# Side products grouped into runs, cheaper norms of k, and refitted plan costs in a float32 DeltaNet/HGRN2 trunk

## Chip, cores and metric

The kernel runs on one core of one Trainium2 chip. The metric is the device time of one launch in microseconds (us). Three runs of the kernel before took 2888.34 to 2891.47 us, median 2890.0.

## What is computed

Two decoder layers over 256 tokens of width 2048, all in float32. Layer 0 mixes tokens with a gated DeltaNet (GDN), layer 1 with HGRN2; a SwiGLU follows each, and an RMSNorm ends the trunk. Cut to what matters here:

```python
def gdn_mixer(h, w_in, ...):                 # 16 key heads, 32 value heads of 128
    proj = h @ w_in                          # k, q, v, z and two gates
    qkv = silu(causal_depthwise_conv(proj[..., :8192], conv_w))
    q, k = l2norm(q) * 128 ** -0.5, l2norm(k)   # x * rsqrt(sum(x * x) + 1e-6)
    A = where(strict, (k b) @ k.T * decay, 0)   # per chunk of 64 tokens
    T = triangular_solve(eye + A, eye)          # its inverse
    ...                                         # o from T, v, decayed q k.T
    return (rmsnorm(o, head_norm) * silu(z)) @ w_out

def swiglu(h, w_gate, w_up, w_down):
    return (silu(h @ w_gate) * (h @ w_up)) @ w_down
```

HGRN2 forms its scores from products of q and k whose decay differs per channel; the kernel builds them in levels (spans of 64, 32, 16, ... tokens).

## The kernel before

**Main stream.** Every weight matrix is read once, in 946 pieces of 512 KB. SyncE issues the reads; ScalarE rounds a piece to fp32r (`wh`), VectorE takes the rest (`wl = raw - wh`). Each float32 product is then three fp32r products of TensorE (high by high, high by low, low by high). Products of weights with the activations go into tiles called `main` (two of them in PSUM), in the fixed order of the groups: for GDN `GDN_ORDER`, where k3, v3 and z3 are the projections of head group 3 (2 key heads, 4 value heads) and o0 to o3 the output projection, each over two head groups; then the FFN, HGRN2, the second FFN. One piece is 12 products of 512 columns or 24 of 256.

**Side products.** All else on TensorE goes into tiles called `aux` (four in PSUM): transposes (`head` holds the identity), scores of k and q (`kqv`), sums of squares (`ones,sq`), the block inverse (`inv`, `u`, `nmat`), outputs (`r`, `w`, `v`, `sc`), HGRN2 scores (`qp`, `kp`, `q_last`).

**Inverse of a head group.** `gdn_qk` multiplies the scores with the decay into `nmat`. `gdn_inverse` (L931) writes its 32x32 diagonal blocks to DRAM (`n_dram`), reads them back spread over the partitions (`wide`, 512 KB), inverts them by 31 pairs of VectorE instructions (the recurrence, `utmp` and `u`), writes the result to DRAM (`u_dram`), reads it into `u`, transposes blocks into `inv` on VectorE, and finishes with 32x32 and 64x64 products on TensorE. The four kinds of transfer stand in one queue, that of POOL, in program order, as do the reads and writes of the residual `x`.

**What sets the order.** All calls are first recorded (`Recorder`), then `plan` (L274) simulates five engines with the costs of `COST`, `LANDING` and `MARGIN` and writes each engine's program in the order that comes out. On TensorE a side product is put ahead of the next main product once its inputs are planned to be ready, plus `HOP` and `PE_SLACK` (1.5 us). The engines then run these lists in order, and wait on semaphores where an input is late. All instructions are issued from one line, L439, so rows are told apart by the names of their tiles.

Of the kernel before, what the change touches and what calls it, by code (L numbers as in the profile page):

```python
# [11 lines left out]
AF = mybir.ActivationFunctionType  # L12
ALU = mybir.AluOpType
PSUM = bass.MemoryType.PSUM
# [3 lines left out]
P = 128  # L18
T = 256
D = 2048  # L20
EPS = 1e-6
CH = 64
# [10 lines left out]
GDN_ORDER = (  # L33
    "k0 k1 v0 z0 v1 k2 z1 k3 v2 z2 v3 k4 o0 z3 k5 v4 k6 o1 v5 k7 z4 z5 v6 z6 v7 z7 o2 o3"
)
# [5 lines left out]
HOP = 0.2  # L41
PE_SLACK = 1.5
FP32_PRODUCT = 0.224
COST = {
    ("vector", "tensor_tensor"): (0.14, 1.08e-3),
    ("vector", "scalar_tensor_tensor"): (0.20, 1.08e-3),
    ("vector", "tensor_scalar"): (0.16, 0.7e-3),
# [6 lines left out]
    ("vector", "reciprocal"): (0.20, 1.0e-3),  # L54
    ("scalar", "activation"): (0.22, 0.83e-3),
# [3 lines left out]
    ("gpsimd", "affine_select"): (0.5, 1.1e-3),  # L59
}  # L60
MARGIN = 1.06
POW = 1.75
LANDING_OF = {"wide": 15.0}
TABLE = {AF.Exp: "exp", AF.Silu: "silu", AF.Sigmoid: "sigmoid", AF.Ln: "ln", AF.Tanh: "exp silu sigmoid"}
# [72 lines left out]
class Recorder:  # L137
# [134 lines left out]


    def plan(self):  # L274
        ops = self.ops
        for op in ops:
            for p in op.pred:
                p.succ.append(op)
# [17 lines left out]
        order = []  # L296
        table = None
        starved = {}
# [45 lines left out]
        while len(order) < len(ops):  # L344
# [15 lines left out]
            if e == "scalar" and op.method == "activation":  # L360
                need = TABLE.get(op.args[2])
                if need and table not in need.split():
                    table = need.split()[0]
                    op.cost += TABLE_LOAD
            self.at[op.n] = at
            order.append(op)
# [84 lines left out]
class Trunk:  # L451
# [162 lines left out]
    def make_xt(self, cg, norm):  # L614
        nc = self.nc
        for pair in range(2):
            ps = self.aux()
            for k in range(2):
                for tt in range(2):
                    nc.tensor.transpose(  # L620
                        ps[:, k * T + tt * P : k * T + (tt + 1) * P],
                        self.x[cg][:, tt, (2 * pair + k) * P : (2 * pair + k + 1) * P],
                        self.ident,
                    )
            for k in range(2):
# [220 lines left out]
    def gdn_qk(self, hg, pre, st):  # L846
# [33 lines left out]
        for kh in range(2):  # L880
# [22 lines left out]
            nc.vector.tensor_scalar(  # L903
                out=ss[:, kh, :], in0=ps1[:, T : T + 4], scalar1=1e-6, scalar2=None, op0=ALU.add
            )
# [95 lines left out]
    def gdn_v(self, hg, pre, st):  # L1001
        nc = self.nc
        v = self.tile(self.pool, [P, 4, T], "kqv")
        self.conv_silu(pre, [32 + 4 * hg + h for h in range(4)], v)
        r = self.tile(self.pool, [P, 2, 4, P], "r")
        for tt in range(2):
            tr = self.aux()
            for h in range(4):
                nc.tensor.transpose(
                    tr[:, h * P : (h + 1) * P], v[:, h, tt * P : (tt + 1) * P], self.ident  # L1010
                )
            for kh in range(2):
# [18 lines left out]
    def head_out(self, o, zs, scale, norm):  # L1031
# [40 lines left out]
        oh, ol = (t([P, 4, T], f"ot_{x}", dt=F32R, bufs=3) for x in "hl")  # L1072
        for b in range(2):
            tr = self.aux()
            for h in range(2):
                for tt in range(2):
                    nc.tensor.transpose(
                        tr[:, h * T + tt * P : h * T + (tt + 1) * P],
                        og[:, tt, (2 * b + h) * P : (2 * b + h + 1) * P], self.ident,
                    )  # L1080
            s = slice(2 * b, 2 * b + 2)
# [189 lines left out]
    def hgrn_scores(self, g, q, st):  # L1271
# [34 lines left out]
        nc.gpsimd.memset(sc, 0.0)  # L1306
        for n, s in enumerate(LEVELS[:-1]):
            e, qp = t([P, 4, T], "e", bufs=2, ordered=True), t([P, 4, P], "qp", bufs=2, ordered=True)
# [16 lines left out]
            tt(qp.rearrange("p h (n s) -> p (h n) s", s=s), qv[:, :, 1, :], ev[:, :, 1, :], ALU.mult)  # L1325
            ps = self.aux()
            for h in range(4):
                for tok in range(2):
# [4 lines left out]
                        qp[:, h, tok * CH : (tok + 1) * CH], start=True, stop=True,  # L1333
                    )
            pv = ps.rearrange("p (a n s) -> p a n s", a=8, s=s)
            if whole:
                for i in range(CH // s):
# [4 lines left out]
            else:  # L1342
# [5 lines left out]
                )  # L1348


        e, qp = t([P, 4, T], "e", bufs=2, ordered=True), t([P, 8, CH + P], "q_last")
# [5 lines left out]
        tt(qp[:, :, 0:CH], qv[:, :, :, 1], ev[:, :, :, 1], ALU.mult)  # L1357
        mask = lambda m: m.unsqueeze(1).broadcast_to([P, 2, m.shape[1]])
        for h in range(4):
            ps = self.aux()  # L1360
            pv = ps[:, 0 : 2 * (CH + P)].rearrange("p (a i) -> p a i", a=2)
            for tok in range(2):
                nc.tensor.matmul(
                    pv[:, tok, :], k[:, h, tok * P : (tok + 1) * P], qp[:, 2 * h + tok, :],
                    start=True, stop=True,
                )
            out = sc[:, 2 * h : 2 * h + 2, :]
            nc.vector.copy_predicated(
                out.rearrange("p a (n t) -> p a n t", t=2)[:, :, :, 1],
                mask(self.masks[:, len(MASKED) - 1, :]), pv[:, :, 0:CH],  # L1370
            )
            nc.vector.copy_predicated(out, mask(self.same), pv[:, :, CH:])
        st["sc"] = sc
# [188 lines left out]
```

## Time and profile before

| | |
|---|---|
| median of three runs | 2890.0 us |
| profiled execution | 2890.57 us |
| its span | 2888.8 us |
| PE / DVE / ACT / POOL busy | 2851.6 / 1717.8 / 1430.9 / 197.3 us |
| mean granted TensorE clock | 0.995 |
| main products | 9024 of 512 columns, 4656 of 256 |
| runs of side products between main products | 350 |

Matmuls overlap, and the end of one is modelled, so durations on PE are not to be added up. The distance from one start to the next is what a product takes in the stream. A product of two float32 operands stands as two records (x8 is four products); a transpose and an fp32r product stand as one.

### The profile page before, as it was taken

The numbers are of one execution on the slowest core, as the hardware profiler recorded it, in microseconds if no ns is written. First come the engines' busy times: TensorE is split into PE (matmuls) and PEld (weight loads), VectorE is DVE, ScalarE is ACT, GpSimd is POOL, SyncE is SP. The second block draws the span as 40 slices with busy tenths as digits, with TensorE's granted clock in tenths as the row PEclk, the third lists the DMA queues.
The fourth block names the chain that finished last, engine by engine and source line by source line (L and its number), as shares of the span: only waits on it lengthen the run. The fifth ranks groups of instructions, "written<-read, shape, count | busy, mean of one in ns | idle before, by whom it ended". The sixth has DMA issues, their size and how long they took to land.

```text
span 2888.8 us, 41300 instructions
## 1 busy us (share of the span) xinstructions
PE 2851.6 (99%) x16074; PEld 2461.4 (85%) x16074; DVE 1717.8 (59%) x2477; ACT 1430.9 (50%) x1998; POOL 197.3 (7%) x286
## 2 busy tenths in 40 slices
PE   8999999999999999999999999999999999999998
PEld 8999979798888888888888989989888888888886
DVE  6777766677755554444445577677665545444454
ACT  6646556456555444434444555556454444344443
POOL 1101111221010000000000100000010000000000
PEclk9999999999999999999999999999999999999999
DMA  7565565755567555666556645445585556665554
GB/s 240 187 190 162 178 193 164 218 169 162 168 224 235 190 189 189 204 229 199 190 189 216 216 148 176 151 148 176 188 283 190 189 188 201 226 205 190 190 199 150
DMA packets 158004, 555.96 MB, mean 192 GB/s; under 512 B 21216, under 2 KB 21360, under 8 KB 157680
## 3 DMA queue, kind: packets, MB, share of 16 engines
q1 hardware_dynamic: 137456, 498.23, 52.7%
q0 software_dynamic: 19264, 53.00, 5.9%
q8 instruction: 126, 2.06, 0.3%
q10 hardware_dynamic: 1088, 2.10, 0.2%
q14 instruction: 70, 0.57, 0.1%
HBM read 530.14 MB, written 23.10 MB: 192 GB/s over the span
## 4 chain that ended last, share of the span: by engine, by line
PE 96%; DMA 2%; issue 1%; DVE 0%; ACT 0%; POOL 0%; ACTq 0%; POOLq 0%; DVEq 0%
PE main L439 88%; PE aux L439 8%; DMA u<-u_dram 1%; DMA u_dram<-u 1%; DMA x<-in_x 0%; ACT wh L439 0%; DVE wl L439 0%; DVE y L439 0%; ACT junk L439 0%; POOL x L439 0%; DVE inv L439 0%; DVE x L439 0%; ACT xt_h L439 0%; ACT kqv L439 0%; DVE xt_l L439 0%
## 5 line engine op out<-in xcount | busy, mean ns | idle before, releaser
L439 DVE TENSOR_TENSOR wl<-raw,wh 128x1024 fp32r<-128x1024 f32 x946 | 1159.3, 1226 | 1045.9 <-ACT wh L439 1045.0
L439 ACT ACTIVATE wh<-raw 128x1024 fp32r<-128x1024 f32 x946 | 1002.7, 1060 | 1294.5 <-PE main L439 1214.1
L439 PE MATMUL main<-wl,xt_h 128*128 128x512 f32 x1920 | 754.7, 393 | 0.0
L439 PE MATMUL main<-wh,xt_l 128*128 128x512 f32 x1920 | 754.7, 393 | 0.0
L439 PE MATMUL main<-wh,xt_h 128*128 128x512 f32 x1920 | 752.4, 392 | 0.0
L439 PE MATMUL main<-xt_h,wh 128*128 128x256 f32 x1552 | 445.4, 287 | 0.0
L439 PE MATMUL main<-xt_l,wh 128*128 128x256 f32 x1552 | 444.2, 286 | 0.0
L439 PE MATMUL main<-xt_h,wl 128*128 128x256 f32 x1552 | 442.8, 285 | 0.2 <-DVE wl L439 0.2
L439 PEld LDWEIGHTS main<-wh,xt_l 128*128 128x128 f32 x1920 | 360.9, 188 | 75.4 <-issue 0.2
L439 PEld LDWEIGHTS main<-wh,xt_h 128*128 128x128 f32 x1920 | 360.7, 188 | 73.7 <-issue 0.7
L439 PEld LDWEIGHTS main<-wl,xt_h 128*128 128x128 f32 x1920 | 360.6, 188 | 73.1 <-issue 0.7
L439 PEld LDWEIGHTS main<-xt_l,wh 128*128 128x128 f32 x1552 | 298.5, 192 | 2.8 <-issue 1.9
L439 PEld LDWEIGHTS main<-xt_h,wh 128*128 128x128 f32 x1552 | 298.5, 192 | 2.0 <-issue 1.2
L439 PEld LDWEIGHTS main<-xt_h,wl 128*128 128x128 f32 x1552 | 298.3, 192 | 1.7 <-issue 0.7
L439 PE MATMUL main<-wl,hth 128*128 128x512 f32 x704 | 274.3, 390 | 0.0
L439 PE MATMUL main<-wh,htl 128*128 128x512 f32 x704 | 274.2, 390 | 0.0
L439 PE MATMUL main<-wh,hth 128*128 128x512 f32 x704 | 274.2, 389 | 0.0
L439 PEld LDWEIGHTS main<-wh,htl 128*128 128x128 f32 x704 | 132.2, 188 | 27.6
L439 PEld LDWEIGHTS main<-wh,hth 128*128 128x128 f32 x704 | 132.2, 188 | 27.4
L439 PEld LDWEIGHTS main<-wl,hth 128*128 128x128 f32 x704 | 132.2, 188 | 27.1
L439 PE MATMUL main<-wh,ot_h 128*128 128x512 f32 x384 | 153.0, 399 | 0.0
L439 PE MATMUL main<-wh,ot_l 128*128 128x512 f32 x384 | 152.4, 397 | 0.0
(181 smaller groups left out, 2196.7 us busy)
## 6 DMA issues: line engine op xcount, KB each, us to landing
raw<-in_ffn_gu SPq DMA_DIRECT2D x352, 512.0 KB, 3.6
raw<-in_ffn_d SPq DMA_DIRECT2D x176, 512.0 KB, 4.2
raw<-in_hgrn_in SPq DMA_DIRECT2D x128, 512.0 KB, 3.6
raw<-in_gdn_kq SPq DMA_DIRECT2D x64, 512.0 KB, 3.8
raw<-in_gdn_v SPq DMA_DIRECT2D x64, 512.0 KB, 4.4
raw<-in_gdn_z SPq DMA_DIRECT2D x64, 512.0 KB, 3.6
raw<-in_gdn_out SPq DMA_DIRECT2D x64, 512.0 KB, 3.9
x_home<-x POOLq DMA_DIRECT2D x36, 512.0 KB, 4.7
```

Of the source, the lines that this page charges most:

```text
L439: getattr(getattr(tc.nc, op.eng), op.method)(*args, **kw)
```

## The change

1. `batches()` runs before the plan: the products into one `aux` tile, or into two tiles that were allocated `together`, are tied so that all become ready for the plan at once, when the last input of any is. Transposes, HGRN2 levels and last-level products are rewritten into such pairs.
2. Norms of k: the sum of squares of k is read off the diagonal of the score product k k^T, with one VectorE instruction per half of the tokens; products with a column of ones remain for q only (two instead of four for each pair of key heads).
3. The plan's costs are refitted (`MARGIN` 1.06 to 1.02, `POW` 1.75 to 1.3, 16 us for `wide`, 7.5 us instead of 6.5 for `u`), and a turn between main and side products gets a price, `TURN`.
4. `GDN_ORDER` is changed.

```diff
 GDN_ORDER = (
-    "k0 k1 v0 z0 v1 k2 z1 k3 v2 z2 v3 k4 o0 z3 k5 v4 k6 o1 v5 k7 z4 z5 v6 z6 v7 z7 o2 o3"
+    "k0 k1 v0 z0 v1 k2 z1 v2 k3 z2 v3 k4 k5 o0 z3 v4 k6 v5 k7 z4 o1 z5 v6 z6 v7 z7 o2 o3"
 )
...
+TURN = 0.06
-    ("vector", "tensor_tensor"): (0.14, 1.08e-3),
+    ("vector", "tensor_tensor"): (0.14, 1.065e-3),
...
-MARGIN = 1.06
-POW = 1.75
-LANDING_OF = {"wide": 15.0}
+MARGIN = 1.02
+POW = 1.3
+LANDING_OF = {"wide": 16.0, "u": 7.5}
...
+    def batches(self):
+        runs = {}
+        for op in self.ops:
+            if op.main or not op.tiles or op.eng == "none":
+                continue
+            v = next((v for v in op.tiles if v.pool.space == PSUM), None)
+            if v is None:
+                continue
+            key = min(w.name for w in v.together if w.pool.space == PSUM)
+            if op.eng != "tensor":
+                runs.pop(key, None)
+                continue
+            run = runs.setdefault(key, [])
+            run.append(op)
+            self.edge(run[0], op)
+            for p, reads in op.pred.items():
+                if p.eng != "tensor" and p is not run[0]:
+                    self.edge(p, run[0], reads)
...
     def plan(self):
+        self.batches()
...
+            if e == "tensor":
+                op.cost += TURN * (op.main != streaming)
+                streaming = op.main
...
     def make_xt(self, cg, norm):
-        for pair in range(2):
-            ps = self.aux()
+        two = self.aux(), self.aux()
+        nc.together(*two)
+        for pair, ps in enumerate(two):
...
     (gdn_qk)
-            sq = t([P, 2, T], "sq")
-            nc.scalar.activation(sq, both, AF.Square)
+            sq = t([P, T], "sq", bufs=2)
+            nc.scalar.activation(sq, both[:, 1, :], AF.Square)
             for tt in range(2):
-                for c in range(2):
-                    at = T + 2 * tt + c
-                    nc.tensor.matmul(
-                        ps1[:, at : at + 1], sq[:, c, tt * P : (tt + 1) * P], self.ones[:, 0:1],
-                        start=True, stop=True,
-                    )
+                nc.tensor.matmul(
+                    ps1[:, T + tt : T + tt + 1], sq[:, tt * P : (tt + 1) * P], self.ones[:, 0:1],
+                    start=True, stop=True,
+                )
+            for tt, ps in enumerate((ps0, ps1)):
+                nc.vector.scalar_tensor_tensor(
+                    out=self.vjunk[:, 0:P], in0=ps[:, 0:P], scalar=1.0, in1=self.ident,
+                    op0=ALU.mult, op1=ALU.mult, accum_out=ss[:, kh, 2 * tt : 2 * tt + 1],
+                )
+            nc.vector.tensor_copy(ss[:, kh, 1:4:2], ps1[:, T : T + 2])
...
     (hgrn_scores)
+        for n in range(0, len(LEVELS) - 1, 2):
+            two = self.aux(), self.aux()
+            nc.together(*two)
+            for step in (products, keep):
+                for i in range(2):
+                    step(n + i, LEVELS[n + i], two[i])
```

What this moves, at three places. On TensorE, the score products of one pair of key heads in head group 4 (`kqv` is k or q after the convolution, `ones,sq` a sum of squares), before and then now:

```order
L439 MATMUL main_5019<-xt_h_12_68,wl_4918 128x256
L439 MATMUL aux_5047<-kqv_4372 128x256
L439 MATMUL aux_5047<-ones_59,sq_4952 128x1 x4
L439 MATMUL aux_5061<-kqv_4372 128x512
L439 MATMUL main_5019<-xt_h_12_68,wh_4900 128x256
```

```order
L465 MATMUL main_5030<-xt_l_17_73,wh_5002 128x256
L465 MATMUL aux_5139<-kqv_4335 128x512
L465 MATMUL aux_5145<-kqv_4335 128x256
L465 MATMUL aux_5145<-ones_59,sq_4419 128x1 x2
L465 MATMUL main_5030<-xt_h_13_69,wl_5015 128x256
```

Four products with ones became two, here and at the 15 other places.

On TensorE, the first products of the inverse of head group 2 (`inv` comes from VectorE's transposes), before and then now:

```order
L439 MATMUL main_4254<-wl_4219,ot_h_321 128x512
L439 MATMUL aux_4303<-inv_3368,nmat_3110 32x32
L439 MATMUL main_4254<-wh_4200,ot_l_322 128x512
L439 MATMUL main_4254<-wh_4227,ot_h_324 128x512
L439 MATMUL main_4254<-wl_4240,ot_h_324 128x512
L439 MATMUL main_4254<-wh_4227,ot_l_325 128x512
L439 MATMUL aux_4303<-inv_3368,nmat_3110 32x32 x15
L439 MATMUL main_4254<-wh_4227,ot_h_324 128x512
```

```order
L465 MATMUL main_4467<-wl_4407,ot_h_323 128x512
L465 MATMUL main_4467<-wh_4391,ot_l_324 128x512
L465 MATMUL main_4467<-wh_4391,ot_h_323 128x512
L465 MATMUL aux_4484<-inv_3290,nmat_3086 32x32 x16
L465 MATMUL main_4467<-wl_4407,ot_h_323 128x512
L465 MATMUL main_4467<-wh_4391,ot_l_324 128x512
```

One product and fifteen, with four main products between, became one run of sixteen. In the whole program 350 runs of side products became 183.

On POOL's queue, the transfers around the inverse of head group 2 (`u_dram_318` and `u_321` are its result on the way out and back, `n_dram_412`/`444` and `wide_414`/`446` the blocks of head group 3, `x` the residual), before and then now:

```order
L439 DMA n_dram_412_4071<-nmat_405_3948 32x8x32 x4
L439 DMA x_615_4110<-in_x 128x2x512
L439 DMA u_dram_318_4144<-u32_320_3132 128x8x32
L439 DMA x_home_1_96<-x_601_448 128x2x512
L439 DMA wide_414_4172<-n_dram_412_4071 128x1x1024
L439 DMA u_321_3524<-u_dram_318_4144 32x8x32 x4
```

```order
L465 DMA n_dram_444_4276<-nmat_437_4036 32x8x32 x4
L465 DMA u_dram_318_4308<-u32_320_3061 128x8x32
L465 DMA wide_446_4364<-n_dram_444_4276 128x1x1024
L465 DMA u_321_3430<-u_dram_318_4308 32x8x32 x4
L465 DMA x_home_1_96<-x_641_418 128x2x512
```

The two transfers of x are gone from between; `wide` of the next head group still stands right ahead of the read of `u`.

## Rows read from the trace of the kernel before

**Rows 1.** The page, engines: busy us, share of the span, instructions.

```profile
PE 2851.6 (99%) x16074; PEld 2461.4 (85%) x16074; DVE 1717.8 (59%) x2477; ACT 1430.9 (50%) x1998; POOL 197.3 (7%) x286
```

**Rows 2.** The page, chain of work that ended last, by engine.

```profile
PE 96%; DMA 2%; issue 1%; DVE 0%; ACT 0%; POOL 0%; ACTq 0%; POOLq 0%; DVEq 0%
```

**Rows 3.** Waits of PE: us in total, times, longest.

```profile
PE aux L439 <- DVE inv L439: 13.7, 3, 7.2
```

**Rows 4.** Timeline of PE, score products with four sums: start, us, what.

```profile
634.09 0.39 PE L439 MATMUL main<-wh,xt_l 128*128 128x512 f32 x1
...
634.54 0.39 PE L439 MATMUL main<-wl,xt_h 128*128 128x512 f32 x1
...
635.20 0.95 PE L439 MATMUL aux<-ones,sq 128*128 128x1 f32 x8
...
637.18 0.40 PE L439 MATMUL main<-wh,xt_h 128*128 128x512 f32 x1
```

**Rows 5.** Timeline of PE, two such score products without sums.

```profile
105.85 0.39 PE L439 MATMUL main<-wh,xt_l 128*128 128x512 f32 x1
106.08 1.45 PE L439 MATMUL aux<-kqv 128*128 128x256 f32 x4
...
107.60 0.40 PE L439 MATMUL main<-wl,xt_h 128*128 128x512 f32 x1
```

**Rows 6.** Timeline of PE, head group 6: inverse products as one and fifteen.

```profile
727.44 0.39 PE L439 MATMUL main<-wl,xt_h 128*128 128x512 f32 x1
727.76 0.24 PE L439 MATMUL aux<-inv,nmat 32*32 32x32 f32 x2
...
728.27 0.40 PE L439 MATMUL main<-wh,xt_h 128*128 128x512 f32 x1
...
729.43 0.40 PE L439 MATMUL main<-wh,xt_l 128*128 128x512 f32 x1
729.75 0.69 PE L439 MATMUL aux<-inv,nmat 32*32 32x32 f32 x30
...
730.71 0.40 PE L439 MATMUL main<-wl,xt_h 128*128 128x512 f32 x1
```

**Rows 7.** Timeline of PE, head group 5: the same products as one run.

```profile
647.03 0.39 PE L439 MATMUL main<-wh,xt_h 128*128 128x512 f32 x1
647.35 0.69 PE L439 MATMUL aux<-inv,nmat 32*32 32x32 f32 x32
...
648.31 0.40 PE L439 MATMUL main<-wh,xt_l 128*128 128x512 f32 x1
```

**Rows 8.** Timeline of DVE, head group 2: end of the recurrence, first and third transpose.

```profile
358.78 0.16 DVE L439 TENSOR_TENSOR u<-u,utmp 128x8 f32<-128x8 f32 x1
...
383.29 0.43 DVE L439 STREAM_TRANSPOSE inv<-u 32x256 f32<-32x256 f32 x1 [8.63 <-DMA u<-u_dram]
...
385.84 0.43 DVE L439 STREAM_TRANSPOSE inv<-u 32x256 f32<-32x256 f32 x1
```

**Rows 9.** Timeline of POOL, head group 2: `wide` of group 3, then `u`.

```profile
363.17 0.74 POOL L439 DMA_DIRECT2D wide<-n_dram  x1
364.88 2.30 POOL L439 DMA_DIRECT2D u<-u_dram  x4 [0.97 <-DMA u_dram<-u]
```

**Rows 10.** The eight transfers into `wide`, whole span: issue to landing.

```profile
DMA to landing us min/median/max: 11.9/14.8/19.7
```

**Rows 11.** Timeline of PE, head group 2: the wait and the products behind it.

```profile
377.58 0.39 PE L439 MATMUL main<-wl,ot_h 128*128 128x512 f32 x1
383.78 0.31 PE L439 MATMUL aux<-inv,nmat 32*32 32x32 f32 x2 [5.81 <-DVE inv L439]
...
384.61 0.63 PE L439 MATMUL main<-wh,ot_h 128*128 128x512 f32 x1
385.04 0.63 PE L439 MATMUL main<-wl,ot_h 128*128 128x512 f32 x1
```

**Rows 12.** Busy time by stretch: engines, then granted clock (PEclk), DMA share.

```profile
380.20:390.40 10.20, 6.62 (x44) 4.98 (x45) 6.50 (x15) 1.81 (x3) 0.73 (x1) 0.50 0.49 162
```

More of the change, by code (lines that the diff above doesn't have):

```diff
@@ L42 @@
 PE_SLACK = 1.5
+TURN = 0.06
 FP32_PRODUCT = 0.224
 COST = {
-    ("vector", "tensor_tensor"): (0.14, 1.08e-3),
-    ("vector", "scalar_tensor_tensor"): (0.20, 1.08e-3),
+    ("vector", "tensor_tensor"): (0.14, 1.065e-3),
+    ("vector", "scalar_tensor_tensor"): (0.205, 1.065e-3),
     ("vector", "tensor_scalar"): (0.16, 0.7e-3),
@@ L54 @@
     ("vector", "reciprocal"): (0.20, 1.0e-3),
-    ("scalar", "activation"): (0.22, 0.83e-3),
+    ("scalar", "activation"): (0.235, 0.82e-3),
     ("gpsimd", "tensor_tensor"): (0.10, 2.3e-3),
@@ L58 @@
     ("gpsimd", "memset"): (0.10, 0.85e-3),
-    ("gpsimd", "affine_select"): (0.5, 1.1e-3),
+    ("gpsimd", "affine_select"): (0.1, 1.05e-3),
 }
-MARGIN = 1.06
-POW = 1.75
-LANDING_OF = {"wide": 15.0}
+MARGIN = 1.02
+POW = 1.3
+LANDING_OF = {"wide": 16.0, "u": 7.5}
 TABLE = {AF.Exp: "exp", AF.Silu: "silu", AF.Sigmoid: "sigmoid", AF.Ln: "ln", AF.Tanh: "exp silu sigmoid"}
@@ L296, in plan @@
         order = []
-        table = None
+        table, streaming = None, False
         starved = {}
@@ L624, in make_xt @@
                     )
+        for pair, ps in enumerate(two):
             for k in range(2):
@@ L893, in gdn_qk @@
             )
-            sq = t([P, 2, T], "sq")
-            nc.scalar.activation(sq, both, AF.Square)
+            sq = t([P, T], "sq", bufs=2)
+            nc.scalar.activation(sq, both[:, 1, :], AF.Square)
             for tt in range(2):
-                for c in range(2):
-                    at = T + 2 * tt + c
-                    nc.tensor.matmul(
-                        ps1[:, at : at + 1], sq[:, c, tt * P : (tt + 1) * P], self.ones[:, 0:1],
-                        start=True, stop=True,
-                    )
+                nc.tensor.matmul(
[8 more added lines that the diff above has]
+            nc.vector.tensor_copy(ss[:, kh, 1:4:2], ps1[:, T : T + 2])
             nc.vector.tensor_scalar(
-                out=ss[:, kh, :], in0=ps1[:, T : T + 4], scalar1=1e-6, scalar2=None, op0=ALU.add
+                out=ss[:, kh, :], in0=ss[:, kh, :], scalar1=1e-6, scalar2=None, op0=ALU.add
             )
@@ L1005, in gdn_v @@
         r = self.tile(self.pool, [P, 2, 4, P], "r")
-        for tt in range(2):
-            tr = self.aux()
+        two = self.aux(), self.aux()
+        nc.together(*two)
+        for tt, tr in enumerate(two):
             for h in range(4):
@@ L1011, in gdn_v @@
                 )
+        for tt, tr in enumerate(two):
             for kh in range(2):
@@ L1072, in head_out @@
         oh, ol = (t([P, 4, T], f"ot_{x}", dt=F32R, bufs=3) for x in "hl")
-        for b in range(2):
-            tr = self.aux()
+        two = self.aux(), self.aux()
+        nc.together(*two)
+        for b, tr in enumerate(two):
             for h in range(2):
@@ L1080, in head_out @@
                     )
+        for b, tr in enumerate(two):
             s = slice(2 * b, 2 * b + 2)
@@ L1306, in hgrn_scores, with products @@
         nc.gpsimd.memset(sc, 0.0)
-        for n, s in enumerate(LEVELS[:-1]):
+        def products(n, s, ps):
             e, qp = t([P, 4, T], "e", bufs=2, ordered=True), t([P, 4, P], "qp", bufs=2, ordered=True)
@@ L1325, in hgrn_scores @@
             tt(qp.rearrange("p h (n s) -> p (h n) s", s=s), qv[:, :, 1, :], ev[:, :, 1, :], ALU.mult)
-            ps = self.aux()
             for h in range(4):
@@ L1334, in hgrn_scores, with keep @@
                     )
+        def keep(n, s, ps):
             pv = ps.rearrange("p (a n s) -> p a n s", a=8, s=s)
-            if whole:
+            if s not in MASKED:
                 for i in range(CH // s):
@@ L1348, in hgrn_scores @@
                 )
+        for n in range(0, len(LEVELS) - 1, 2):
+            two = self.aux(), self.aux()
+            nc.together(*two)
+            for step in (products, keep):
+                for i in range(2):
+                    step(n + i, LEVELS[n + i], two[i])
         e, qp = t([P, 4, T], "e", bufs=2, ordered=True), t([P, 8, CH + P], "q_last")
@@ L1358, in hgrn_scores @@
         mask = lambda m: m.unsqueeze(1).broadcast_to([P, 2, m.shape[1]])
+        pv = []
         for h in range(4):
-            ps = self.aux()
-            pv = ps[:, 0 : 2 * (CH + P)].rearrange("p (a i) -> p a i", a=2)
+            if h % 2 == 0:
+                two = self.aux(), self.aux()
+                nc.together(*two)
+            pv.append(two[h % 2][:, 0 : 2 * (CH + P)].rearrange("p (a i) -> p a i", a=2))
             for tok in range(2):
                 nc.tensor.matmul(
-                    pv[:, tok, :], k[:, h, tok * P : (tok + 1) * P], qp[:, 2 * h + tok, :],
+                    pv[h][:, tok, :], k[:, h, tok * P : (tok + 1) * P], qp[:, 2 * h + tok, :],
                     start=True, stop=True,
                 )
+        for h in range(4):
             out = sc[:, 2 * h : 2 * h + 2, :]
@@ L1369, in hgrn_scores @@
                 out.rearrange("p a (n t) -> p a n t", t=2)[:, :, :, 1],
-                mask(self.masks[:, len(MASKED) - 1, :]), pv[:, :, 0:CH],
+                mask(self.masks[:, len(MASKED) - 1, :]), pv[h][:, :, 0:CH],
             )
-            nc.vector.copy_predicated(out, mask(self.same), pv[:, :, CH:])
+            nc.vector.copy_predicated(out, mask(self.same), pv[h][:, :, CH:])
         st["sc"] = sc
```

## The prediction

> **What bounds the kernel now.** I read the page's engine line, its chain, then PE's waits, then PE's timeline at the places the change touches, and last DVE and POOL around the waits. The reader is to see that TensorE is the bound for the whole span: it is busy 99% [rows 1], and 96% of the chain that ended last is PE [rows 2]. VectorE, at 59%, and ScalarE, at 50%, have room. So a microsecond counts if PE issues less, or waits less. It waits little, and nearly all in one place: 13.7 us in three waits for `inv`, VectorE's transposes ahead of the block inverse, 7.2 us the longest [rows 3].
>
> Durations on PE overlap, so I work with starts. In the stream a 512-column main product takes 0.227 us (634.09 to 634.54 holds two [rows 4]). What a run of side products costs is the distance of the main products around it, less 0.227 for each main product in it.
>
> **Norms of k.** From 634.54 to 637.18 is 2.64 us, with two main products: 2.19 us for a run with two score products and four sums [rows 4]. The run without sums goes from 105.85 to 107.60, 1.75 us, also with two: 1.30 us [rows 5]. Four products with a column of ones thus take 0.89 us, one 0.22. Two of four go at each of 16 places, 32 in all: 32 x 0.223 = **7.1 us**, all on the bound engine. In their place VectorE gets two products with the diagonal mask of 128 columns and a small copy per place, under 1 us each time, some 15 us over the program. Its 41% of idle time [rows 1] covers that; without the cover it would lengthen the way to `nmat`, which PE awaits only tens of microseconds later.
>
> **Runs instead of single products.** Where the 32x32 products stand as one and fifteen, the lone one costs 728.27 - 727.44 - 2 x 0.227 = 0.38 us and the fifteen 730.71 - 729.43 - 2 x 0.227 = 0.83 [rows 6]. One run of sixteen costs 647.03 to 648.31, 1.28 - 0.45 = 0.83 [rows 7]. So a second run of these costs 0.38 however little is in it. In the order there were 15 such pairs (7 of `inv`, 8 of `u,pp`), now none. Two stand in the waits below and are counted there: 13 x 0.38 = **4.9 us**. The other 152 runs that disappear (350 less 183 less 15) are mostly transposes and outputs of full width, and no row here gives them such a price; the bounds are zero and 0.38 for each of the 12 HGRN2 score runs of 64 columns among them, 4.6 us. I take a value near the lower end, as most are wide: **1 us**.
>
> **The waits for the inverse.** In head group 2 the recurrence ends at 358.9, the third transpose at 386.3 [rows 8]. PE has its next place at 377.8 and starts at 383.8 [rows 11]: the list allowed 18.9 us where 24.9 were needed for the first transpose and 27.3 for the third. The cause is in the queue: `wide` of the next group is issued at 363.2, `u` at 364.9 [rows 9], and `u` lands when the transpose starts, at 383.3. That is 18.4 us after its issue, and 20.1 after `wide`. A transfer into `wide` takes 14.8 us in the median and up to 19.7 [rows 10]. The reader is to see that `u` is small and late only because `wide` is ahead of it. After the wait the granted clock is 0.50, that is 1.2 GHz, for 10.2 us in which PE is busy 6.6 [rows 12], and main products take 0.43 (384.61 to 385.04 [rows 11]) instead of 0.227. At 2.4 GHz half of the 6.6 us would do: about 3 us more. The longest wait, 7.2 us, is in head group 4 and is built alike. Together: 13.7 + 2 x 2.7, taking a little off for what is not full-rate work, **19 us**.
>
> What does the change make of it? Counted in the order, from the piece behind whose split the recurrence ends on VectorE to the piece in which PE has its first 32x32 product, the eight distances were 3.0 to 5.0 pieces, mean 4.15, and are 4.2 to 5.9, mean 5.06. A piece is 12 x 0.227 = 2.7 us, so PE comes 2.4 us later; as a count by pieces is coarse I take 2, and 18.9 becomes 20.9. In POOL's list the read of `u` has a `wide` directly ahead of it in head groups 2 and 6 now; in head group 4 it has none any more. In group 2 two transfers of x have gone from between, so `wide` goes out between some 1.5 us after the recurrence (right behind the write of `u_dram`; `u` itself followed `wide` by 1.7 [rows 9]) and the 4.3 of before (363.2 - 358.9). From there 14.8 to 19.7 for `wide`, 0.4 until `u` lands, 3.0 for the transposes (383.3 to 386.3): 19.7 to 27.4, against 20.9. The wait is 0 to 6.5 us. The median of `wide` is likelier than the longest, which shared the queue with x: 2.5. In group 6 the blocks are written earlier, 15 VectorE rows before the recurrence ends instead of 7, so `wide` follows the write closely: 1.5 to 2.5, then as above, 19.7 to 25.6, a wait of 0 to 4.7, taken as 1. Half clock behind two shorter waits is not in the trace: 0 to 3 each; I take 1 in all. Left over: 4.5 us. Gained: 19 - 4.5 = **14.5 us**.
>
> Later places on PE could be late too, since the costs are lower: 1.06 to 1.02 is 4%, on chains of a few microseconds between two side products a tenth or two, against 1.5 us of `PE_SLACK`, which stays. I count nothing. The new order of projections moves main products among themselves, each as long as before: nothing.
>
> **A rule against it.** [rows 9] show `u`, issued 1.7 us behind `wide`, landing after it. The Trainium skill, "DMA: Bandwidth & Descriptors", section "Queues, rings and completion order", says that each DMA engine takes descriptors in the order of the ring; a later transfer of one queue then can't overtake. By that rule alone the two pairs `wide`, `u` in the new list would cost what the two of before cost; that is the first rival. The trace agrees in the one case shown; it doesn't show how much the later place of PE takes off.
>
> **Sum.** 7.1 + 4.9 + 1 + 14.5 = 27.5 us off the profiled execution, 2890.57 (span 2888.8 and 1.8 around it): 2863.1. The median of the runs, 2890.0, is 0.6 lower: **2862.5 us**.
>
> **Rivals.**
> - *The waits stay.* Two `u` reads stand behind `wide` as before, and cost 19 us again. For it: the list; against: PE's later place, the x transfers gone. 2890.0 - 13.0 = 2877.
> - *The waits go altogether.* `wide` near its shortest, 11.9 us [rows 10], or `u` ahead by luck: 2890.0 - 13.0 - 19 = 2858. Against: two pairs still stand so.
> - *The tighter plan is late everywhere at the inverse* (slower). With lower costs VectorE's transposes end after PE's place in all eight head groups, and each time the clock halves as in [rows 12]: 8 x (6 + 3) = 72 us in place of 19, so 2890.0 - 13.0 - 19 + 72 = 2930. It makes the kernel slower from (13.0 + 19) / 8 = 4.0 us per head group. For it: the transposes stand in VectorE's line behind splits and recurrences. Against: the distances grew.
> - *Nothing moves*: the products removed were hidden behind weight loads or waits, and runs cost no turn. 2890. Against: the starts in [rows 4, 5] are real time on PE.
>
> **Chances.** Forecast 0.58, waits stay 0.20, waits go 0.14, slower 0.04, nothing 0.04. The measurement tells 0.2%, 5.8 us, from no change. Faster takes the first three and a little of the last: 0.92; same 0.04; slower 0.04. The forecast's own range, from waits of 0 to 10 us left over and 0 to 4.6 for the other runs, is 2854 to 2869. The range reaches to both first rivals: 2856 to 2878.
>
> **What the profile would show.** The sums: `ones,sq` with 64 records instead of 128, and a run with scores and two sums at 1.75 us instead of 2.19. The runs: `inv` and `u,pp` of 32x32 always x32, at 0.83. The waits: PE for `inv` below 6 us in all, in head groups 2 and 6 only, none at 4; the clock at 0.50 shorter than 10 us or not at all. I am wrong if PE waits for anything else by more than 3 us, if `u` lands behind `wide` in more than two groups, or if main products wait for `wl` or `ot`.

## The result, and the profile after

The changed kernel takes 2857.12 us in the median of four runs (2856.47 to 2859.76), the kernel before 2890.73 beside it: ratio 0.9886, 95% interval 0.9869 to 0.9903. The profiled execution took 2856.91 us, its span is 2855.2.

The page's engine line, TensorE first (busy us, share, instructions): 21.7 us less on PE than in [rows 1], 64 records fewer; VectorE has 12 us more and still idles 39%.

```profile
PE 2829.9 (99%) x16010; PEld 2451.5 (86%) x16010; DVE 1730.1 (61%) x2557; ACT 1428.9 (50%) x2000; POOL 195.2 (7%) x286
```

The waits of PE (us in total, times, longest). Of the 13.7 us for `inv` in [rows 3], 1.9 are left. The wait for `first` at the start of the program is 8.8 us in the kernel before and nearly the same in all.

```profile
PE aux L465 <- DMA first<-in_x: 8.7, 2, 6.1
PE aux L465 <- DVE inv L465: 1.9, 2, 1.3
PE aux L465 <- ACT kqv L465: 0.7, 1, 0.7
```

PE's timeline at score products with two sums, where [rows 4] have four. From 434.24 to 436.43 are 2.19 us with two main products of 512 columns, so the run costs 2.19 - 0.45 = 1.74 us. Reckoned the same way, the run with four sums in [rows 4] cost 2.64 - 0.45 = 2.19.

```profile
434.24 0.39 PE L465 MATMUL main<-wl,xt_h 128*128 128x512 f32 x1
434.47 1.45 PE L465 MATMUL aux<-kqv 128*128 128x512 f32 x4
435.76 0.50 PE L465 MATMUL aux<-ones,sq 128*128 128x1 f32 x4
436.12 0.48 PE L465 MATMUL main<-wh,xt_l 128*128 128x512 f32 x1
436.43 0.28 PE L465 MATMUL main<-xt_h,wh 128*128 128x256 f32 x1
```

Head group 2, where TensorE waited 5.81 us in [rows 11]. First VectorE (last step of the recurrence, the transposes), then POOL's queue, then PE.

```profile
361.82 0.17 DVE L465 TENSOR_TENSOR u<-u,utmp 128x8 f32<-128x8 f32 x1
...
380.19 0.90 DVE L465 STREAM_TRANSPOSE inv<-u 32x256 f32<-32x256 f32 x2
...
382.44 0.43 DVE L465 STREAM_TRANSPOSE inv<-u 32x256 f32<-32x256 f32 x1
```

```profile
362.54 0.92 POOL L465 DMA_DIRECT2D u_dram<-u  x1 [1.04 <-DVE acc L465]
363.45 0.74 POOL L465 DMA_DIRECT2D wide<-n_dram  x1
366.59 2.31 POOL L465 DMA_DIRECT2D u<-u_dram  x4 [2.40 <-DMA u_dram<-u]
```

```profile
381.93 0.39 PE L465 MATMUL main<-wh,ot_h 128*128 128x512 f32 x1
382.25 0.69 PE L465 MATMUL aux<-inv,nmat 32*32 32x32 f32 x32
382.88 0.50 PE L465 MATMUL main<-wl,ot_h 128*128 128x512 f32 x1
383.21 0.40 PE L465 MATMUL main<-wh,ot_l 128*128 128x512 f32 x1
```

From issue to landing, that `wide` alone (the DMA issues of 350 to 400 us; KB, us):

```profile
wide<-n_dram POOLq DMA_DIRECT2D x1, 512.0 KB, 16.4
```

`u` still lands behind `wide`: the first of its four reads at 380.2, when the first transpose starts. But that is now 18.2 us after the end of the recurrence (362.0), not 24.4: `wide` went out 1.5 us after that end instead of 4.2, and took 16.4 us instead of 19.7. TensorE has its place 20.3 us after the recurrence, not 19.0 (383.78 less its wait of 5.81, less 358.94). So it does not wait: the sixteen products need the first two transposes, which end at 381.1; the third ends at 382.9, when the products are done. The same ten microseconds as in [rows 12], by stretch, have the granted clock at 1.00 where it was 0.50:

```profile
380.20:390.40 10.20, 10.20 (x104) 7.80 (x102) 9.92 (x18) 5.65 (x8) 1.55 (x3) 1.00 0.82 274
```

What is left is in head group 0. There the write of `u_dram` stands behind `wide` of the next group; first POOL's queue, then PE, whose granted clock stays at 1.00:

```profile
182.68 0.72 POOL L465 DMA_DIRECT2D wide<-n_dram  x1 [20.08 <-DVE utmp L465]
183.39 0.94 POOL L465 DMA_DIRECT2D u_dram<-u  x1
```

```profile
204.38 0.24 PE L465 MATMUL aux<-inv,nmat 32*32 32x32 f32 x2 [0.61 <-DVE inv L465]
205.96 0.69 PE L465 MATMUL aux<-inv,nmat 32*32 32x32 f32 x30 [1.33 <-DVE inv L465]
```

### The profile page after: what moved, and what is told of

Its sections match the earlier page's. It is cut to its first block, busy times and chain, and to the rows that moved or that the text cites. A ratio compares the mean times of both kernels' runs of the same rounds, so it can differ in the third digit from the quotient of the medians.

```text
span 2855.2 us, 41255 instructions
## 1 busy us (share of the span) xinstructions
PE 2829.9 (99%) x16010; PEld 2451.5 (86%) x16010; DVE 1730.1 (61%) x2557; ACT 1428.9 (50%) x2000; POOL 195.2 (7%) x286
## 4 chain that ended last, share of the span: by engine, by line
PE 97%; DMA 1%; ACT 0%; DVE 0%; issue 0%; POOLq 0%; POOL 0%; DVEq 0%; ACTq 0%
PE main L465 90%; PE aux L465 7%; DMA u_dram<-u 1%; DMA raw<-in_gdn_v 0%; DMA first<-in_x 0%; ACT wh L465 0%; DMA u<-u_dram 0%; DVE wl L465 0%; DVE y L465 0%; ACT dec L465 0%; ACT junk L465 0%; ACT L465 0%; DVE x L465 0%; ACT zs L465 0%; DVE acc L465 0%
## 5 line engine op out<-in xcount | busy, mean ns | idle before, releaser
L465 PEld LDWEIGHTS main<-wl,hth 128*128 128x128 f32 x704 | 132.2, 188 | 27.4
L465 PEld LDWEIGHTS main<-wh,htl 128*128 128x128 f32 x704 | 132.2, 188 | 27.4
```

Of the source, the lines that this page charges most:

```text
L465: getattr(getattr(tc.nc, op.eng), op.method)(*args, **kw)
```

## A ledger by starts

The experiments below give many traces, and I count one way in all of them. PE's program is cut into stretches of main and of side products; each costs the distance to the start of the next. From that goes what its products take in an undisturbed stream (0.227 us for 512 columns, 0.120 for 256, 0.112 for a transpose, 0.223 for a float32 product of up to 128 columns, 0.05 for 32x32, and so on): "products" in the table. The excess is split. "Waits" are the gaps of PE over 0.45 us from 25 us to the end of GDN; "half clock" is half of PE's busy time where the granted clock is 0.50 there; "turns" is the remainder (only its differences mean something); "start" the first 25 us. Some 20 us, 6 ahead of the first product and 14 behind the last, are nearly the same in all. The time is the median of the runs; the other columns come from the one execution that was profiled, which lies up to 4.6 us from that median (2894.2 in e5, 2892.4 in e9, 2885.3 in e11).

| kernel | time | products | start | waits | half clock | turns |
|---|---|---|---|---|---|---|
| before | 2890.7 | 2831.6 | 6.6 | 13.7 | 6.1 | 10.6 |
| after | 2857.1 | 2824.4 | 5.4 | 2.6 | 0 | 2.6 |
| e1 norms alone | 2901.8 | 2824.4 | 6.8 | 24.6 | 10.6 | 12.4 |
| e2 runs alone | 2892.4 | 2831.6 | 6.8 | 18.8 | 12.2 | 2.9 |
| e3 costs and order alone | 2879.6 | 2831.6 | 7.1 | 3.7 | 3.3 | 10.5 |
| e4 before, `wide` behind `u` | 2882.6 | 2831.6 | 6.9 | 7.2 | 1.7 | 13.9 |
| e5 after, old costs | 2889.6 | 2824.4 | 6.4 | 26.1 | 11.3 | 4.5 |
| e6 after, old order | 2878.8 | 2824.4 | 6.5 | 16.3 | 7.5 | 2.3 |
| e7 after, `wide` behind `u` | 2860.7 | 2824.4 | 5.4 | 3.4 | 1.7 | 2.4 |
| e8 norms, runs, `wide` behind `u` | 2888.0 | 2824.4 | 7.1 | 22.7 | 8.8 | 4.1 |
| e9 norms and runs | 2896.6 | 2824.4 | 6.8 | 25.8 | 9.5 | 4.1 |
| e10 after, old transfer times | 2860.2 | 2824.4 | 6.0 | 2.6 | 3.3 | 1.8 |
| e11 after, old MARGIN and POW | 2889.2 | 2824.4 | 7.5 | 18.3 | 8.0 | 5.7 |
| e12 after, 9 us for `u` | 2863.5 | 2824.4 | 6.4 | 5.5 | 2.8 | 3.3 |

From before to after: products 7.1, start 1.2, waits 11.1, half clock 6.1, turns 8.0; together 33.5, and the spans differ by 33.6.

## The experiments

**e1, norms alone.** Of the change only `gdn_qk` is taken:

```diff
-            sq = t([P, 2, T], "sq")
-            nc.scalar.activation(sq, both, AF.Square)
+            sq = t([P, T], "sq", bufs=2)
+            nc.scalar.activation(sq, both[:, 1, :], AF.Square)
...
+                nc.vector.scalar_tensor_tensor(
+                    out=self.vjunk[:, 0:P], in0=ps[:, 0:P], scalar=1.0, in1=self.ident,
```

> The kernel before with the norms of k by diagonal sums and nothing else of the change: 32 of the 64 products with a column of ones go, the plan's costs, the order of projections and the single products stay. Theory (the prediction's first term): the products with ones are real time on TensorE, 32 x 0.223 = 7.1 us; a score run of two products with two sums takes 1.75 us instead of 2.19, at all 16 places. With the waits for inv as before, about 2883.5. Rival, nothing moves: the removed products lay beside weight loads or waits, score runs keep 2.2 us or the main products behind them get longer: 2890. Second rival, the order: any edit moves the plan, and the waits for inv change by chance; then the time differs from 2883.5 by just what the waits for inv in the trace differ from 13.7 us plus the half clock behind them. In POOL's list wide still stands between the write and the read of u in three head groups, so I expect these waits to stay.

2901.82 us against 2891.9, ratio 1.0032 (1.0019 to 1.0044): 0.3% slower, which is small but outside the noise. The products are 7.1 us less; the waits and the half clock went from 19.8 to 35.2. PE's waits, and two of its four stretches at half clock (busy us of each engine, then the granted clock):

```profile
PE aux L439 <- DVE inv L439: 14.3, 4, 5.9
...
PE aux L439 <- DVE og L439: 4.8, 1, 4.8
PE main L439 <- ACT ot_h L439: 2.2, 2, 1.5
```

```profile
410.46:417.28 6.82, 3.25 (x16) 3.18 (x16) 3.66 (x6) 1.08 (x2) 0.00 (x0) 0.50 0.24 76
...
857.60:864.43 6.83, 5.10 (x15) 3.76 (x16) 3.83 (x11) 1.37 (x2) 0.99 (x1) 0.50 0.01 2
```

The products column is a count by a price. That the price is real shows in this trace itself: the thirteen score runs with two sums that have no other side product beside them cost 1.74 us each, and those with four in the kernel before 2.18 to 2.20. It shows in the turns, too, which don't take the 7.1 us back (after has 2.6; e2, the same runs with the old norms, 2.9; in e1 they rose by 1.8). So the saving is real and the time hides it: a few instructions changed the plan, and new waits took more than was saved. That is the second rival in its kind, but not as it was put: the waits for `inv` grew by 0.6 us only, those for other tiles by over 10, and the half clock by 4.5.

**e2, runs alone.** `batches()` and the pairs of tiles, nothing else:

```diff
     def plan(self):
+        self.batches()
...
-            ps = self.aux()
+        two = self.aux(), self.aux()
+        nc.together(*two)
```

> The kernel before with the runs alone: products into one tile or a pair of tiles tied together, transposes and HGRN2 levels in pairs; old costs, old order of projections, old norms. Side runs on TensorE: 182 instead of 350, and 16 runs of 32x32 products instead of 31. Theory of the prediction: 13 split 32x32 runs x 0.38 = 4.9 us and 1 us for the other runs, so 2884 with the waits for inv as before (19 us). Rival 1, a run costs more than I took: the whole difference of after by starts, about 9 us, is runs, and the time is 2881 with the waits as before. Rival 2: a run that has to be ready as a whole comes later on TensorE, and that alone is what removed the waits for inv; then they fall below 5 us here and the time is near 2866.

2892.38 against 2891.9, ratio 1.0001 (0.9992 to 1.001). Turns fell by 7.7 us (10.6 to 2.9), more than the 5.9 that I had given them, and near rival 1; waits and half clock rose by 11.2. Rival 2 falls: runs alone don't remove the waits.

```profile
PE aux L461 <- DVE inv L461: 9.9, 5, 4.4
```

**e3, costs and order alone.**

```diff
-    "k0 k1 v0 z0 v1 k2 z1 k3 v2 z2 v3 k4 o0 z3 k5 v4 k6 o1 v5 k7 z4 z5 v6 z6 v7 z7 o2 o3"
+    "k0 k1 v0 z0 v1 k2 z1 v2 k3 z2 v3 k4 k5 o0 z3 v4 k6 v5 k7 z4 o1 z5 v6 z6 v7 z7 o2 o3"
...
+TURN = 0.06
...
-MARGIN = 1.06
-POW = 1.75
-LANDING_OF = {"wide": 15.0}
+MARGIN = 1.02
+POW = 1.3
+LANDING_OF = {"wide": 16.0, "u": 7.5}
...
```

> The kernel before with the refitted costs, the price of a turn and the new order of projections alone: 327 side runs, 31 of them with 32x32 products, all 64 products with ones. Theory: TensorE's later place at the inverse and the shorter POOL list come from the plan, so the waits for inv fall below 5 us here, the half clock behind them goes, and the time is 2890 - 15 = 2875. Rival 1, it is the runs that made the waits go: they stay near 13.7 us, and the time is 2890. Rival 2, the tighter plan by itself is late elsewhere (MARGIN 1.02): waits of TensorE for tiles other than inv by more than 5 us, slower than 2890.

2879.62, ratio 0.9954 (0.9941 to 0.9966); 2875 was expected. Products and turns are those of before; the waits for `inv` are 3.7 us instead of 13.7, and from 25 us on nothing else waits by more than 0.45 us:

```profile
PE aux L443 <- DVE inv L443: 3.7, 2, 2.5
```

The theory holds in its direction: the plan's numbers alone, costs and order together, remove most of the waits, for 12 us instead of the 15 expected. To the time of the changed kernel the norms and the runs are lacking.

**e4, the queue's order.** The kernel before, with `wide` kept behind the `u` of the group before:

```diff
+        nc.wanted = self.last_u
         nc.gpsimd.dma_start(
             nrep, n_dram.rearrange("n j i -> n (j i)").unsqueeze(0).broadcast_to([4, 32, 1024])
         )
...
         st["u"] = um
+        self.last_u = [nc.ops[-1]]
```

> The kernel before, with one thing put in the plan: the read of wide of the next head group may be issued only behind the reads of u of the group before. All else, costs, order, runs and norms, is as before (339 side runs, 32 with 32x32 products). Theory: u is late because wide, 512 KB, is ahead of it in POOL's queue. Without it u lands 5 to 6 us after its issue instead of 18, the waits for inv go (below 2 us), no half clock in the head groups, and the time is 2890 - 17 = 2873; wide comes some 3 us later, which nothing awaits. Rival 1: u is late for itself (VectorE behind, or the transfer slow with other traffic); the waits stay near 13.7 us and the time near 2890. Rival 2: the later wide delays the next recurrence, and the wait comes back one head group later.

2882.6, ratio 0.9966 (0.9952 to 0.9979). No wait for `inv` is left. The writes and reads of `u_dram` (one row for all 40: min, median, max from issue to landing) take at most 8.0 us, where `u` took 18.4 in head group 2 before (383.3 less 364.9, [rows 8, 9]); in head group 4, which had the longest wait, POOL's list now has `wide` behind it:

```profile
DMA to landing us min/median/max: 2.1/3.9/8.0
```

```profile
537.38 0.91 POOL L439 DMA_DIRECT2D u_dram<-u  x1
...
542.64 2.31 POOL L439 DMA_DIRECT2D u<-u_dram  x4 [1.86 <-issue]
...
550.91 0.74 POOL L439 DMA_DIRECT2D wide<-n_dram  x1 [0.44 <-issue]
```

```profile
PE main L439 <- ACT ot_h L439: 3.5, 2, 2.5
PE aux L439 <- DVE og L439: 3.0, 1, 3.0
```

So the cause named in the prediction is shown: `u` was late because `wide` was ahead of it. The traces without this edit say the same: in the eleven kernels that lack it, the write or the reads of `u` were issued 37 times while a `wide` was under way, and each time they landed behind it, by 0.3 to 6.4 us. The Trainium skill ("DMA: Bandwidth & Descriptors", section "Queues, rings and completion order") says, where it describes the queues of SyncE and ScalarE, that each DMA engine consumes descriptors in the order of the ring, but that a later one may finish its write before an earlier one. The 37 landings on POOL's queue agree with the order; that a later transfer can't overtake, as the prediction concluded, does not follow from the section, though no run here shows one that did.

But 17 us were expected and 9 came: elsewhere in the plan new waits for `og` and `ot_h` arose, and turns rose by 3.3.

**e5 and e6, the changed kernel with one half of the plan's numbers put back**: in e5 the costs (the price of a turn with them), in e6 the order of projections.

```diff
-TURN = 0.06
...
-MARGIN = 1.02
-POW = 1.3
-LANDING_OF = {"wide": 16.0, "u": 7.5}
+MARGIN = 1.06
+POW = 1.75
+LANDING_OF = {"wide": 15.0}
...
```

> The changed kernel with the costs of before (MARGIN 1.06, POW 1.75, 15 us for wide, 6.5 for u, no price of a turn); runs, norms and the new order of projections stay. In the two runs that had the old costs and the old order with norms or runs new, TensorE waited 14.3 and 9.9 us for inv and some 5 us for og of the last head group, each with half clock behind it, which gave back all that the norms and the runs had saved. Theory: the refitted costs are what makes these waits go, since they tell the plan how late u really is. Here they are missing, wide still stands between write and read of u in head groups 4 and 6, so waits for inv and og of 10 to 18 us and half clock behind them: 2857 + 20, near 2877. Rival, the new order of projections makes them go: 2859 or less, waits below 4 us.

```diff
-    "k0 k1 v0 z0 v1 k2 z1 v2 k3 z2 v3 k4 k5 o0 z3 v4 k6 v5 k7 z4 o1 z5 v6 z6 v7 z7 o2 o3"
+    "k0 k1 v0 z0 v1 k2 z1 k3 v2 z2 v3 k4 o0 z3 k5 v4 k6 o1 v5 k7 z4 z5 v6 z6 v7 z7 o2 o3"
```

> The changed kernel with the order of projections of before; refitted costs, runs and norms stay. Theory, the costs make the waits go: waits for inv and og below 5 us in all, 2857 to 2864. Rival, the order makes them go: waits of 10 to 18 us with half clock behind them, near 2877. The list on POOL has wide between the write and the read of u in head groups 2 and 4, not in 6, as many as the kernel before has; if the place in the queue alone decided, the time would be near 2875.

e5 took 2889.6 (ratio 0.9991, 0.9983 to 0.9999), e6 2878.75 (0.9949, 0.9937 to 0.9961). I had expected one of the two to carry the gain; both are needed. Without the costs 32.5 us of it are lost, without the order 21.6, of 33.6 in all. In e6, POOL's queue in head group 2 shows a worse form of the same fault. POOL waits for the recurrence (`utmp`), which still reads the one buffer of `wide`, and sends the next `wide`; `u_dram` stands behind it. `u` goes out only when `u_dram` has landed, 20.3 us after the end of the recurrence (380.32 less 360.0):

```profile
358.64 0.73 POOL L465 DMA_DIRECT2D wide<-n_dram  x1 [2.38 <-DVE utmp L465]
...
360.92 0.91 POOL L465 DMA_DIRECT2D u_dram<-u  x1
...
380.32 2.33 POOL L465 DMA_DIRECT2D u<-u_dram  x4 [0.47 <-issue]
```

```profile
PE aux L465 <- DVE inv L465: 11.0, 6, 4.6
...
PE aux L465 <- DVE og L465: 5.3, 2, 4.8
```

**e7, the edit of e4 in the changed kernel.**

> The changed kernel, with the read of wide of the next head group put behind the reads of u of the group before. In the kernel before this took all three waits for inv away (13.7 us to none) and saved 9 us, some given back by new waits for og and ot_h. In the changed kernel only 1.9 us of wait for inv are left. Theory: nothing left to gain here, 2854 to 2858, TensorE waits for inv 0 to 0.5 us, u on the way 5 to 7 us in all groups. Rival, the shifted list makes a new wait for og or ot_h as in the kernel before: 2858 to 2866.

2860.69 (ratio to before 0.9891, 0.9876 to 0.9905; after had 0.9886, 0.9869 to 0.9903, so the two are not told apart). The wait for `inv` is gone, and `og` of the last head group waits 3.4 us instead, as the rival had it:

```profile
PE aux L465 <- DVE og L465: 3.4, 2, 2.8
```

The changed kernel gains nothing from this edit.

**e8, norms and runs with the edit of e4**, in the old plan.

> The kernel before with the norms and the runs of the change, old costs and old order, and the read of wide put behind the reads of u. It says whether the queue's order can take the place of the refitted costs. With the norms (7.1 us) and the runs (about 9) as real savings and no waits for inv: 2891 - 7 - 9 - 17 = 2858 if nothing else waits; with the wait for og of the last head group that three runs with the old costs showed (3 to 5 us, and half clock behind it): 2861 to 2867. Rival, norms and runs were no savings (each alone gave 2902 and 2892): 2882, as with the queue's order alone.

2887.97 (0.9986, 0.9978 to 0.9995). The time lies above all that was expected, the rival included. Products and turns show the savings, no `inv` waits, and yet 31.5 us of waits and half clock: 9.2 for `ot_h`, 7.6 for `og`, 4.4 for `u`. Mending the one queue does not replace the refit.

**e9, norms and runs in the old plan**. With e5, e6 and the changed kernel it completes a square: old or new costs by old or new order, all four with norms and runs.

> The changed kernel with both the costs and the order of projections of before: norms and runs alone, together. With the changed kernel, the one with old costs (2890) and the one with old order (2879) it closes a square. Theory: norms (7.1 us) and runs (8 us by the starts outside the waits) are real, but a plan with the old costs leaves TensorE 20 to 37 us of waits and half clock in the head groups whatever else is changed (20, 31, 35 and 37 so far); in POOL's list wide stands between u_dram and u in head groups 2, 4 and 6. So 2854 + 20 to 37: 2874 to 2891, with a wait for og of the last head group near 4.8 us. Rival: norms and runs together are enough to move TensorE's places behind u; waits below 6 us and 2860.

2896.61 (1.0015, 1.0006 to 1.0024), a little slower than before and than I had expected. From here the new costs alone gain 18 us (e6), the new order alone 7 (e5), both 39 (after). PE's waits:

```profile
PE aux L461 <- DVE inv L461: 11.8, 8, 2.8
...
PE aux L461 <- DVE og L461: 5.3, 2, 4.8
PE main L461 <- ACT ot_h L461: 4.8, 1, 4.8
```

**e10 to e12, single costs in the changed kernel**: the old transfer times; the old MARGIN and POW; a longer time for `u`.

```diff
-LANDING_OF = {"wide": 16.0, "u": 7.5}
+LANDING_OF = {"wide": 15.0}
```

> The changed kernel with the two transfer times of before alone (15 us for wide, and the general 6.5 us for u instead of 7.5). In POOL's list u_dram or u then stands behind wide only in head group 0. Theory A, the place in the queue relative to the end of the recurrence decides: little wait, 0 to 4 us in head group 0, 2856 to 2862. Theory B, the later place of TensorE that the 7.5 us give is what hides the waits: TensorE comes 1 us earlier in all groups, waits for inv in several of them, 2862 to 2875. Under either a wait for og of the last head group may come, 5 to 10 us with the half clock.

2860.16 (0.9886, 0.9872 to 0.9899): no difference from after. One place waits, head group 0, where `u_dram` is behind `wide`:

```profile
187.20 0.73 POOL L465 DMA_DIRECT2D wide<-n_dram  x1 [2.35 <-DVE u L465]
187.93 0.94 POOL L465 DMA_DIRECT2D u_dram<-u  x1
204.57 2.32 POOL L465 DMA_DIRECT2D u<-u_dram  x4 [15.70 <-DMA u_dram<-u]
```

The time and the waits are those of Theory A. The run shows that few waits can be had without the 7.5 us for `u`. It does not show what a later place of TensorE is worth: the list changed with the number, and in head groups 2 and 6 `u` is now ahead of `wide`, so there was no wait to hide.

```diff
-MARGIN = 1.02
-POW = 1.3
+MARGIN = 1.06
+POW = 1.75
```

> The changed kernel with MARGIN 1.06 and POW 1.75 of before and all other new numbers kept. In POOL's list u_dram stands behind wide in head groups 0, 2 and 4, and u behind wide in head group 6. Theory: MARGIN shifts the recurrence against wide of the next head group; with four groups behind wide the waits for inv come back, 8 to 15 us and half clock behind them, 2865 to 2882. Rival: the landing of 7.5 us for u is enough to keep TensorE's place late, waits below 4 us and 2857 to 2860.

2889.24 (0.9987, 0.9979 to 0.9996), slower than even the theory had it: these two numbers alone give back nearly all. The waits are many and mostly not for `inv`:

```profile
PE aux L465 <- DVE og L465: 6.3, 3, 4.8
PE aux L465 <- DVE inv L465: 3.7, 3, 2.7
PE main L465 <- DVE wl L465: 2.8, 3, 0.9
PE main L465 <- DVE ot_l L465: 2.0, 1, 2.0
```

```diff
-LANDING_OF = {"wide": 16.0, "u": 7.5}
+LANDING_OF = {"wide": 16.0, "u": 9.0}
```

> The changed kernel with 9.0 us instead of 7.5 for u in the plan, nothing else. TensorE's place at the inverse comes 1.5 us later. In POOL's list u stands behind wide in head group 2, u_dram behind wide in head groups 0, 4 and 6. Theory B, the later place hides the landing: no waits for inv, 2854 to 2857, a version a little faster than the changed one. Theory A, the queue decides: u_dram behind wide costs the landing of wide and then u's own 4 to 5 us, some 23 to 25 us against a budget near 22, so 1 to 3 us of wait in three groups and half clock: 2862 to 2872.

2863.53 (0.9905, 0.9892 to 0.9919). The time is within Theory A's range, but not by its mechanism: PE waits 1.6 us only for `inv`, and 4.2 for `og` of the last head group. In head groups 0, 4 and 6, where `u_dram` stands behind `wide`, PE waits 0.2 us at most: the first transpose starts 19.6 to 21.1 us after the recurrence, and PE has its place at 21.6 to 21.8. The products need the second transpose, too, which ends at 21.3, 20.6 and 22.1 there; with a place one microsecond earlier, near those of the changed kernel (20.0 to 20.9 in its groups 0, 2 and 6), PE would have waited for it in groups 0 and 6. So the later place helps to hide the landing, as Theory B had it; the gain is lost to `og`.

```profile
PE aux L465 <- DVE og L465: 4.2, 2, 3.7
PE aux L465 <- DVE inv L465: 1.6, 2, 1.4
```

## Why the prediction was right, and where it was not

**Norms: right.** 7.1 us predicted, 7.1 in the products of every kernel that has them; the run is 1.74 us (1.75 predicted), and 64 records of sums are gone.

**Runs: too small.** Predicted 4.9 for the split 32x32 products and 1 for the other 152 runs, measured 8.0 (7.7 in e2). Within GDN, where the split pairs are, 4.8 of it; behind GDN, where TensorE waits in neither trace, 90 runs fewer gave 3.2, of which the HGRN2 levels 2.2. The mis-sized term is the 1 us, taken near the lower end of 0 to 4.6: the HGRN2 runs cost about half of that bound. Runs of full width were nearly free, as assumed: 44 runs of transposes (`head,h`) fewer gave 0.5 us.

**Waits: the size nearly right, the places and the reason only in part.** Predicted gain 14.5 (19 less 4.5 left), measured 17.2 (19.8 less 2.6). That waits stay in groups 2 and 6 was wrong: they are in group 0, and group 4 has none, as said. `u` is behind `wide` in groups 2 and 6 as the list showed. Group 0 was overlooked, because only reads of `u` right behind a `wide` were looked for: there the write is behind it, in the kernel before, too (its third wait, 0.65 us). So one of the signs of being wrong came true, as `u` lands behind `wide` in three groups and not in two, and it cost 1.9 us. The other failing step is the time needed for the transposes. I counted to the end of the third, with 3.0 us behind the landing of `u`, and took a middle of 19.7 to 27.4. But this run of products waits for the first two only: in head group 0 after, its first product starts 0.06 us after the first transpose and its second 0.06 us after the second, and in head group 2 the run is over when the third transpose ends. To the second it was 19.1 us there (381.09 less 361.99), and to the third 20.9, against TensorE's place at 20.3. That place came 1.2 us later (20.3 less 19.0) instead of 2, and over the eight head groups 1.0 in the mean, so the count by pieces had this term at twice its size. These two errors run against each other, and a wait was put into the wrong groups, so that the size came out near owes something to luck. The total is therefore nearer to the rival in which the waits go altogether (2858) than to the forecast (2862.5).

**"I count nothing" for the rest of the plan: right for this kernel as a sum, wrong as a reason.** I treated four edits as if their terms added. In the old plan norms and runs, worth 15 us by the ledger, make the kernel slower (e9), and costs and order alone gain 12 (e3), but together they gain 34. What the plan decides is 2.6 us of waits and half clock or 37. I had put the fewer waits down to TensorE's later place and the shorter list; e10 has them few without the 7.5 us, and e11 many with it, while in e12 the later place helps to hide two landings. The rival "tighter plan late everywhere" had the sign wrong: the plan with the higher costs is the late one (e11, e5).

**A start 1.2 us shorter** was in no term. The sum of the corrections: 2.1 (runs) + 2.7 (waits) + 1.2 = 6.0, from 27.5 to 33.5.

**What goes with the waits of the last head group.** `og` waits in the kernels in which the last recurrence ends late against the main products left to cover the work behind it. From its end to the start of the last product of the output projection there are 108 us before, 109 after, 115 in e10, 142 in e3, and no wait; in the ten others, with 89 to 103 us, the first `og` product of the last head group waits 2.8 to 5.1 us, as here in e1:

```profile
859.32 1.93 PE L439 MATMUL aux<-head,og 128*128 128x128 f32 x7 [4.83 <-DVE og L439]
```

The last recurrence ends at 753.6 in after and at 802.9 in e11, whose instructions are the same. No run moved this distance alone, so it is seen and not proven. Open, too: which of MARGIN and POW does it, why 4% on the planned costs of VectorE, ScalarE and GpSimd (or the price of one operation, POW) puts the chain of head groups 50 us back, and why `wide` took 16.4 us in head group 2 instead of 19.7. Two edits were not tried that might remove the fault in the queue: a second buffer for `wide`, which would let it go out before the recurrence ends, and another form of its read. It is written as a broadcast with the four copies as outer dimension and takes 14.8 us in the median [rows 10], while a 512 KB read of weights on SyncE's queue took 3.7 in the median (before).

## What to carry to other kernels

Where a planner writes the order, split the time into work and waits by starts before judging an edit: a saving on the bound engine can be real and the kernel slower. Refit the planner's costs against a trace in the same step, and try costs and order together; here each alone showed less than half. A small transfer whose result the bound engine awaits shouldn't be queued behind a large one; but mend that together with what comes next on the chain.

## What the runs showed of the hardware

Behind a 512 KB read in POOL's queue a 128 KB write took 12.7 to 19.0 us (18.8 in e6, head group 2: 360.9 to 379.7), and a 32 KB read 11.1 to 18.4 (18.4 before); with none ahead all took 2.1 to 8.0 (e4). In none of the 37 cases did the small transfer land first.

In GDN TensorE waited 37 times for 1.8 us or more in the fourteen traces. In 34 of them the granted clock stood at 0.50 during the wait or right behind it, for 3.4 to 13.7 us; it did not in one wait of 2.5 us (e4), one of 1.9 (e5) and one of 2.1 (e9). Shorter waits went either way: behind two of 0.6 and 1.3 us the clock stayed at 1.00 (after), behind two of 0.9 and 1.3 it was 0.50 for 3.4 us (e6). By the ledger the half clock cost up to 12.2 us in one kernel (e2), two thirds of the waits themselves.
